# A delta-net stage whose TensorE order is planned at build time: three edits to the planner and one rank on VectorE

## The chip, the cores and the metric

The kernel runs on one core of one Trainium2 chip. The metric is the device time of one launch in microseconds (us); lower is better. TensorE (PE in the rows of the profile) does the matmuls, VectorE (DVE), ScalarE (ACT) and GpSimd (POOL) the elementwise work, and SyncE (SP) issues most of the DMAs. Each engine works through its own list of instructions in order.

## The reference, cut to what matters

A trunk of two layers over a sequence of 1024 rows of width 1024, all in f32. Each layer is a mixer and a convolutional FFN, each behind a modulation that is computed from a condition vector. The mixer of layer 0, which the change is about, is a gated DeltaNet with eight heads:

```python
e = jax.nn.silu(c @ cond_w + cond_b)
for i in range(DEPTH):
    mod = (e @ ada_w[i] + ada_b[i])[:, None, :]
    sh1, sc1, g1, sh2, sc2, g2 = jnp.split(mod, 6, axis=-1)
    y = mixers[i % N_MIXERS](x * (1.0 + sc1) + sh1)
    x = layer_norm(DN_ALPHA * x + (1.0 + g1) * y, ln_g[i, 0], ln_b[i, 0])
    y = conv_ffn(x * (1.0 + sc2) + sh2, ffn_up[i], ffn_conv_w[i], ffn_conv_b[i], ffn_down[i])
    x = layer_norm(DN_ALPHA * x + (1.0 + g2) * y, ln_g[i, 1], ln_b[i, 1])
...
# gated_deltanet, per head and chunk
qkv = jax.nn.silu(causal_dwconv(qkv, conv_w))
decay = jnp.where(causal, jnp.exp(jnp.where(causal, diff, 0.0)), 0.0)
kk = jnp.where(strict, jnp.einsum('bhncd,bhnmd->bhncm', kb, k) * decay, 0.0)
sol = lax.linalg.triangular_solve(kk + eye, rhs, left_side=True, lower=True, unit_diagonal=True)
qk = jnp.where(causal, jnp.einsum('bhncd,bhnmd->bhncm', q, k) * decay, 0.0)
_, o = lax.scan(step, state0, xs)
o = o * lax.rsqrt(jnp.mean(o * o, axis=-1, keepdims=True) + 1e-6) * norm_w
o = o * jax.nn.silu(z)
return o @ w_out
```

## The kernel before, in words

Products of two f32 operands in the projections are split into high and low parts and take three matmuls each (`wh`, `wl`, `hT`). The DeltaNet stage runs from about 88 to 640 us of the span. Its heads go in four pairs, with chunks of 128 rows (eight per head). The steps of a pair are generators, and a cooperative loop, `run` (L639), decides at build time in which order TensorE gets their matmuls: it keeps a modelled clock, `clk`, to which each matmul adds its cost, and a generator that yields a number is asked again when that much modelled time has gone by. The numbers are in the table `LAT` (how long the other engines or a DMA are expected to take); among the generators that are due, that with the lowest priority number goes next. `pq` (L625) pins this order for TensorE. On the other engines the instructions stand as a list scheduler puts them, which goes by priority.

The generators that matter here:

- `filler` projects q, k, v and z for all heads (128x512 matmuls `acc<-hT,wh` and `acc<-hT,wl`); their convolution ends on VectorE in L449. After each of its items it executes up to two *modulation steps*, if no solve is in its recursion (`busy`). A modulation step loads two pieces of 256 KB of `ada_w` (L213, into the two buffers `xT`) and adds them up on VectorE (`ada`, L221 for the first, L223 for the seven others). After four steps TensorE transposes the vector (L233), ScalarE sums it (L235, four) and VectorE adds the bias (L237 or L239). There are 24 such steps, six groups with eight VectorE operations each, for the modulation vectors 4, 3 and 2 of layer 0.
- `t_front` (pairs 0 to 3) makes the decay of a head (`decay`, with L740 on VectorE), writes it to DRAM (`Ld`, L751), and computes k times k for each half head: four matmuls into one of the two `mm` banks, then a chain of short VectorE operations on that bank, L766 to L776.
- `t_solve` inverts the diagonal 32x32 blocks, once for pairs 0 and 1 ("first solve") and once for pairs 2 and 3 ("second solve"): a recursion of 31 steps on VectorE, each L800 and L802, then the transposes L806 and L810 with ScalarE's copy L808 between them.
- `t_chain` of a pair copies the results apart on ScalarE (L849, L838) and then has TensorE combine the blocks, beginning with 32x32 matmuls `mm<-T,U`.
- `prep` transposes v and k (`mm<-cst,qkv`) and scales them on VectorE (L914, L923).
- `dt_half(p, q4)` loads half of a pair's decays back (L941, `DT<-Ld`, two loads), then yields `LAT["ld"]`, then does the matmuls of k and q (four per head, `mm<-qkv`), which VectorE multiplies with the loaded decay (L949). For `q4` of 0 the buffer is one of the four `lane` buffers, which the solve uses too.
- `scan` runs the recurrence over the chunks, and `tail` normalises its output.

Behind the stage come the gate (L1130), the gain row g1 (L1622 makes four diagonal matrices from half of modulation vector 2, L1623 turns them into rows, for each of the two halves) and the output projection (L327 to L329): 96 matmuls into the four accumulators for the first half of the columns, which VectorE empties with L357 (times g1), then the second half.

Of the kernel before, what the change touches and what calls it, by code (L numbers as in the profile page):

```python
# [12 lines left out]
ALU = mybir.AluOpType  # L13
# [14 lines left out]
ALPHA = 4.0 ** 0.25  # L28
BAL = {"r11": 0, "r12": 0, "r22": 0, "rS1": 0, "rS2": 0, "rS3": 0, "rS4": 0, "rw21": 0, "rwT1": 0, "rwT2": 0, "rwT3": 0, "rwT4": 0, "rn": 0, "rh": 1, "011": 0, "012": 0, "022": 0, "0S1": 0, "0S2": 0, "0S3": 0, "0S4": 0, "0w21": 0, "0wT1": 0, "0wT2": 0, "0wT3": 0, "0wT4": 0, "0n": 1, "0h": 0, "f11": 0, "f12": 0, "f22": 0, "fS1": 0, "fS2": 0, "fS3": 0, "fS4": 0, "fw21": 0, "fwT1": 0, "fwT2": 0, "fwT3": 0, "fwT4": 0, "fn": 1, "fh": 0, "gw": 0, "gh": 0, "gn": 3, "b1": 0, "b2": 0, "b3": 0, "b4": 0, "bT": 0, "ba": 0, "rw11": 0, "rw22": 0, "0w11": 0, "0w22": 0, "fw11": 0, "fw22": 0}
# [4 lines left out]
def trunk_kernel(ctx: ExitStack, tc, A):  # L34
# [645 lines left out]
    def q4s(q4):  # L680
        return slice(q4 * 4, (q4 + 1) * 4)
# [48 lines left out]
    def decay(h):  # L730
        for q4 in range(2):
            yield from take("t2", 2)
            gm = [tl("t2", [P, 4, P], F32R, name="gm") for _ in range(2)]
            for t, g in zip(gm, (gh64, gl64)):
                pool.tensor_tensor(t, bm(m_incl, 4), bc(g[:, q4s(q4), h], P), ALU.mult)
            yield LAT["gm"]
            pt = mm_tile()
            pm(pt, m_lowr, gm[1], start=True, stop=False)
            pm(pt, m_lowr, gm[0], start=False, stop=True)
            dve.tensor_tensor(U[h][:, q4s(q4)], v4(pt), bm(mneg, 4), ALU.add)  # L740
            give("t2", 2)

    def t_front(p):
        yield after_ev(("g",), ("Tq", p // 2 - 1))
        for h in pairs[p]:
            yield from take("aux", 1)
            U[h] = tl("aux", [P, NCH, P], name="U")
            yield from decay(h)
# [3 lines left out]
        for h in pairs[p]:  # L752
# [4 lines left out]
            for q4 in range(2):  # L757
# [5 lines left out]
                for c in range(4):  # L763
                    n = q4 * 4 + c
                    junk = tl("S", [P, P], name="jk")
                    dve.scalar_tensor_tensor(junk, pt[:, c * P:(c + 1) * P], 1.0, ident, ALU.mult, ALU.mult,  # L766
                                             accum_out=sk[:, n:n + 1])
                qs = q4s(q4)
                dve.tensor_scalar(sk[:, qs], sk[:, qs], 1e-6, None, ALU.add)
                dve.reciprocal(cj[h][:, qs], sk[:, qs])  # L770
                dve.tensor_tensor(cj[h][:, qs], cj[h][:, qs], beta[:, qs, h], ALU.mult)
                if q4:
                    pool.tensor_tensor(ir[h], sk, phalf, ALU.pow)
                for c in range(4):
                    n = q4 * 4 + c
                    dve.scalar_tensor_tensor(U[h][:, n], pt[:, c * P:(c + 1) * P], cj[h][:, n:n + 1],  # L776
                                             U[h][:, n], ALU.mult, ALU.mult)
# [149 lines left out]
    def dt_half(p, q4):  # L927
# [14 lines left out]
        yield LAT["ld"]  # L942
# [101 lines left out]
    busy, owed = [], [0]  # L1044

    def filler(items):
        spare = [(z, k) for k in range(GH)]
        todo = list(items)
        while todo or spare:
# [40 lines left out]
            for _ in range(0 if busy else min(owed[0], 2)):  # L1090
                bg_step(acc_tile)
                owed[0] -= 1

    LAT = {"kk": 3.05, "ld": 1.14, "g1": 17.30, "gm": 2.50, "mm": 1.81, "T": 4.98, "X": 3.38, "fs": 2.2, "T0": 5.00, "t1": 1.65, "t2": 2.35, "t3": 1.34, "D": 2.67, "s1": 1.60, "s2": 1.22, "s3": 1.26, "tail": 12.31, "ssq": 9.30, "fv": 2.85}
# [13 lines left out]
    run(todo)  # L1108
    zearly = list(range(GH))
# [883 lines left out]
```

## Time and profile before

| what | value |
|---|---|
| median of 3 runs | 2937.22 us (2934.47 to 2940.39) |
| the profiled execution: time, span | 2931.49 us, 2929.3 us |
| mean granted clock of TensorE | 0.989 of full speed |
| busy TensorE, VectorE, ScalarE | 2808.1, 2198.4, 1316.2 us |
| VectorE's idle time ahead of L223 (140 of them, all layers) | 27.0 us |

The profiled execution lies 5.7 us under the median. A row of the timeline has the start in the span and the length in us, engine, line, operation, output and inputs with buffer numbers left out, and how many instructions the row stands for; in brackets stands how long the engine was idle ahead of it and whose end released it. A row of waits has the sum in us, how often, and the longest. A row of grouped lines ends with busy time, the mean in ns, and the idle time ahead.

### The profile page before, as it was taken

Reading aid. Unit: us, or ns where it says so; the run is one execution under the profiler, and the core shown is the slowest. Engines: PE = TensorE matmul, PEld = TensorE weight load, DVE = VectorE, ACT = ScalarE, POOL = GpSimd, SP = SyncE. Lnnn points to the kernel's source line nnn. Section 1 sums busy time; section 2 is a strip of 40 time slices with the busy share of each in tenths; the row PEclk is TensorE's granted clock in tenths of the full one; section 3 lists DMA queues with packets and bytes.
Section 4 is the critical chain, followed back from the end, with each engine's and each line's share of the span. In section 5 each row is a group of like instructions: output and inputs, shape, how many; then the busy total and the mean of one; then the engine's idle time right before and its main releaser. Section 6 shows DMA issues by size and latency. Waiting matters only on the chain. (4 is left out here: it accounts for less than half of the span.)

```text
span 2929.3 us, 38823 instructions
## 1 busy us (share of the span) xinstructions
PE 2808.1 (96%) x13638; PEld 2296.3 (78%) x13638; DVE 2198.4 (75%) x3965; ACT 1316.2 (45%) x2457; POOL 421.1 (14%) x485
## 2 busy tenths in 40 slices
PE   8998999999999999999999999999999899999997
PEld 7777877887778888887787877777778688888786
DVE  6695687556788888897687766666697887778888
ACT  3755465443544444536443332221345544444443
POOL 0311220134011111100000000223201011111001
PEclk9999999999999999999999999999999999999999
DMA  8122221354344444863434454555564233335753
GB/s 309 64 80 80 98 91 44 105 187 148 108 150 159 163 157 147 316 218 123 157 110 173 149 181 149 165 172 163 189 235 155 94 137 108 108 108 202 262 158 119
DMA packets 239234, 442.35 MB, mean 151 GB/s; under 512 B 22848, under 2 KB 76352, under 8 KB 239040
## 3 DMA queue, kind: packets, MB, share of 16 engines
q1 hardware_dynamic: 206832, 387.96, 39.4%
q10 hardware_dynamic: 29760, 43.00, 4.0%
q0 software_dynamic: 2448, 8.91, 0.8%
q8 instruction: 107, 1.75, 0.2%
q14 instruction: 87, 0.71, 0.1%
HBM read 331.26 MB, written 108.53 MB: 150 GB/s over the span
## 5 line engine op out<-in xcount | busy, mean ns | idle before, releaser
L1466 PE MATMUL acc<-bb,ab 128*128 128x512 f32 x1800 | 427.5, 393 | 6.5 <-DVE pa L1441 2.5
L1466 PEld LDWEIGHTS acc<-bb,ab 128*128 128x128 f32 x1800 | 338.0, 189 | 81.4 <-DVE bb L90 3.8
L630 PE MATMUL acc<-hT,wh 128*128 128x512 f32 x960 | 300.3, 394 | 0.0
L1605 POOL TENSOR_TENSOR o<-o 128x512 f32<-128x512 f32 x88 | 121.1, 1387 | 810.6 <-DVE o L1598 680.4
L89 ACT ACTIVATE ab<-ar 128x512 fp32r<-128x512 f32 x210 | 129.0, 624 | 184.2 <-PE acc L1466 93.3
L1159 PE MATMUL acc<-T,wb 128*128 128x512 f32 x840 | 204.2, 392 | 7.2 <-DVE wb L90 7.2
L630 PEld LDWEIGHTS acc<-hT,wh 128*128 128x128 f32 x960 | 183.0, 191 | 34.0
L630 PE MATMUL acc<-hT,wl 128*128 128x512 f32 x480 | 202.8, 422 | 0.8 <-DVE qkv L993 0.5
L1159 PEld LDWEIGHTS acc<-T,wb 128*128 128x128 f32 x840 | 157.9, 189 | 43.7 <-DVE wb L90 11.1
L90 DVE TENSOR_TENSOR ab<-ar,ab 128x512 fp32r<-128x512 f32 x210 | 146.4, 703 | 44.2 <-ACT ab L89 44.2
L90 DVE TENSOR_TENSOR wb<-mm,wb 128x512 fp32r<-128x512 f32 x216 | 145.2, 684 | 23.4 <-ACT wb L89 21.7
L90 DVE TENSOR_TENSOR wb<-wr,wb 128x512 fp32r<-128x512 f32 x162 | 111.3, 688 | 65.7 <-ACT wb L89 63.8
L1225 ACT ACTIVATE pc<-acc 128x512 f32<-128x512 f32 x143 | 84.7, 592 | 160.5 <-PE acc L1159 91.6
L89 ACT ACTIVATE wh<-wr 128x1024 fp32r<-128x1024 f32 x101 | 107.0, 1061 | 110.2 <-PE acc L630 50.3
L89 ACT ACTIVATE wb<-mm 128x512 fp32r<-128x512 f32 x216 | 122.3, 593 | 72.8 <-DVE mm L1205 72.1
L90 DVE TENSOR_TENSOR wl<-wr,wh 128x1024 fp32r<-128x1024 f32 x85 | 105.5, 1241 | 61.2 <-ACT wh L89 59.1
L89 ACT ACTIVATE wb<-wr 128x512 fp32r<-128x512 f32 x162 | 99.7, 627 | 96.5 <-DMA wr<-in_ffn_up 53.0
L449 DVE SCALAR_TENSOR_TENSOR qkv<-raw,vc,qkv 128x512 f32<-128x512 f32 x144 | 112.3, 783 | 34.8 <-ACT qkv L447 30.7
L630 PE MATMUL acc<-wh,hT 128*128 128x512 f32 x384 | 135.5, 415 | 0.7 <-DVE vv L90 0.7
L1584 DVE SCALAR_TENSOR_TENSOR o<-g,vc,o 128x512 f32<-128x512 f32 (+2 forms) x176 | 135.2, 786 | 0.7
L223 DVE SCALAR_TENSOR_TENSOR ada<-mvw,e,ada 128x512 f32<-128x512 f32 x140 | 105.9, 757 | 27.0 <-DMA mvw<-in_ada_w 26.5
L110 PE MATMUL acc<-T,wb 128*128 128x512 f32 x292 | 116.6, 399 | 9.9 <-DVE wb L90 9.4
(626 smaller groups left out, 6876.5 us busy)
## 6 DMA issues: line engine op xcount, KB each, us to landing
wr<-in_ffn_up SPq DMA_DIRECT2D x96, 512.0 KB, 4.3
ad<-o SPq DMA_DIRECT2D x154, 256.0 KB, 2.2
ar<-ad SPq DMA_DIRECT2D x154, 256.0 KB, 4.2
mvw<-in_ada_w SPq DMA_DIRECT2D x48, 512.0 KB, 5.5
Br<-in_ffn_down SPq DMA_DIRECT2D x66, 256.0 KB, 3.3
mvw<-in_ada_w SPq DMA_DIRECT2D x64, 256.0 KB, 3.0
wr<-in_ret_wv SPq DMA_DIRECT2D x32, 512.0 KB, 4.2
ar<-od SPq DMA_DIRECT2D x56, 256.0 KB, 5.0
```

The source lines that it names most:

```text
L89: act.activation(dst_h, src, AF.Copy)
L90: eng.tensor_tensor(dst_l, src, dst_h, ALU.subtract)
L110: mm(acc, wl[:, k], hl[0], start=first, stop=False)
L223: dve.scalar_tensor_tensor(a, wr[kk], e[:, k:k + 1], a, ALU.mult, ALU.add)
L449: dve.scalar_tensor_tensor(oh, raw[:, 3 - j:515 - j], w[:, 3 - j:4 - j], oh, ALU.mult, ALU.add)
L630: pq(pe.matmul(out, lhsT, rhs, start=start, stop=stop, **kw), cost)
L1159: return pe.matmul(*a, skip_group_check=True, **kw)
L1225: act.activation(t, X, AF.Copy)
L1466: mm_ = (lambda *a, p=p, onto=onto, **kw: (mm if p < 2 else pe.matmul)(*a, skip_group_check=onto, **kw))
L1584: dve.scalar_tensor_tensor(tv, gv[:, c0 - j:c1 - j], w[:, 2 - j:3 - j], tv, ALU.mult, ALU.add)
L1605: pool.tensor_tensor(o[d], o[x], o[y], op)
```

## The change

Four edits. First, the table gets an entry `ld0` of 7.00, which `dt_half` yields after the loads of `q4` of 0 of the even pairs, in place of 1.14; so the planner puts these matmuls later. Second, a list `fronts` holds the fronts that are running, and `filler` executes no modulation step while it holds any. Third, the VectorE operations L740 and L766 to L776 (and GpSimd's power between them) are issued with a priority that is 80 higher, for the list scheduler. Fourth, modulation steps that are left when `run` ends are executed at once, ahead of the gate phase.

```diff
+RANK = 80
...
     def decay(h):
...
-            dve.tensor_tensor(U[h][:, q4s(q4)], v4(pt), bm(mneg, 4), ALU.add)
+            with tc.high_priority(RANK):
+                dve.tensor_tensor(U[h][:, q4s(q4)], v4(pt), bm(mneg, 4), ALU.add)
...
     def t_front(p):
         yield after_ev(("g",), ("Tq", p // 2 - 1))
+        fronts.append(p)
...
+                with tc.high_priority(RANK):
                     for c in range(4):
...
+        fronts.remove(p)
         emit(("A", p), LAT["kk"])
...
     def dt_half(p, q4):
...
-        yield LAT["ld"]
+        yield LAT["ld"] if p % 2 or q4 else LAT["ld0"]
...
-    busy, owed = [], [0]
+    busy, owed, fronts = [], [0], []
...
     def filler(items):
...
-            for _ in range(0 if busy else min(owed[0], 2)):
+            for _ in range(0 if busy or fronts else min(owed[0], 2)):
                 bg_step(acc_tile)
...
     run(todo)
+    while bg:
+        bg_step()
```

Line numbers of the changed kernel are higher: by 1 up to the first half of `decay`, by 2 to 7 behind it. What moves is shown at three places.

The first is TensorE's order around the first `mm<-T,U`, that of pair 0. Before, with all four groups of four `mm<-qkv` ahead of it (the second eight of them here):

```order
L630 MATMUL mm<-qkv 128x128 x8
L633 MATMUL mm<-cst,qkv 128x128 x8
L633 MATMUL acc<-cst,qkv 128x128 x8
L630 MATMUL acc<-hT,wl 128x512
L630 MATMUL acc<-hT,wh 128x512 x2
L633 MATMUL mm<-cst,qkv 128x128 x8
L630 MATMUL acc<-hT,wl 128x512
L630 MATMUL acc<-hT,wh 128x512 x2
L630 MATMUL acc<-hT,wl 128x512
L630 MATMUL acc<-hT,wh 128x512 x2
L630 MATMUL mm<-T_1923,U 32x32 x32
```

The same place after, with the second and the third group of four:

```order
L631 MATMUL mm<-qkv 128x128 x4
L634 MATMUL mm<-cst,qkv 128x128 x8
L631 MATMUL acc<-hT,wl 128x512
L631 MATMUL acc<-hT,wh 128x512 x2
L631 MATMUL acc<-hT,wl 128x512
L631 MATMUL acc<-hT,wh 128x512 x2
L634 MATMUL acc<-cst,qkv 128x128 x8
L631 MATMUL mm<-qkv 128x128 x4
L634 MATMUL mm<-cst,qkv 128x128 x8
L631 MATMUL acc<-hT,wl 128x512
L631 MATMUL acc<-hT,wh 128x512 x2
L631 MATMUL mm<-T_1896,U 32x32 x32
```

The groups of four have moved apart, and the fourth stands behind the `mm<-T,U`.

The second is VectorE's order where the second solve begins (`Y` is its transposed input, `fs` and `T` are the recursion's tiles). Before:

```order
L449 SCALAR_TENSOR_TENSOR qkv<-raw,vc,qkv 128x512
L792 STREAM_TRANSPOSE Y<-X 128x1024
L449 SCALAR_TENSOR_TENSOR qkv<-raw,vc,qkv 128x512
L800 TENSOR_TENSOR fs<-Y,T 128x31
L449 SCALAR_TENSOR_TENSOR qkv<-raw,vc,qkv 128x512
L802 TENSOR_TENSOR T<-T,fs 128x31
L449 SCALAR_TENSOR_TENSOR qkv<-raw,vc,qkv 128x512
L800 TENSOR_TENSOR fs<-Y,T 128x60
```

And after (L222 and L224 are the former L221 and L223, L805 and L807 the former L800 and L802):

```order
L238 SCALAR_TENSOR_TENSOR v_3820<-cs,vc 128x4
L222 TENSOR_SCALAR ada<-mvw,e 128x512
L797 STREAM_TRANSPOSE Y<-X 128x1024
L450 SCALAR_TENSOR_TENSOR qkv<-raw,vc,qkv 128x512
L224 SCALAR_TENSOR_TENSOR ada<-mvw,e,ada 128x512
L805 TENSOR_TENSOR fs<-Y,T 128x31
L450 SCALAR_TENSOR_TENSOR qkv<-raw,vc,qkv 128x512
L224 SCALAR_TENSOR_TENSOR ada<-mvw,e,ada 128x512
L807 TENSOR_TENSOR T<-T,fs 128x31
```

One group of modulation operations, which stood in the front of pair 3 before, now stands between the first steps of this recursion. The group that stood in the first solve has left it likewise.

The third is TensorE's order in the output projection (`hl` is the gated output, `dg` the diagonal matrices of the gain row). Before, at the projection's tenth matmul:

```order
L329 MATMUL acc<-wh,hl 128x512
L327 MATMUL acc<-wh,hl 128x512
L1623 MATMUL mm<-dg,ones 128x128 x4
L328 MATMUL acc<-wl,hl 128x512
L329 MATMUL acc<-wh,hl 128x512
```

After, behind the 96th:

```order
L329 MATMUL acc<-wl,hl 128x512
L330 MATMUL acc<-wh,hl 128x512
L234 MATMUL mm<-cst,ada 128x128 x4
L1630 MATMUL mm<-dg,ones 128x128 x8
L328 MATMUL acc<-wh,hl 128x512
L329 MATMUL acc<-wl,hl 128x512
```

The last modulation group (L234, the former L233) and the gain row that needs it have moved behind the first half.

More of the change, by code (lines that the diff above doesn't have):

```diff
@@ L762, in t_front @@
                     pm(pt[:, c * P:(c + 1) * P], ks, ks)
[L763 to L777, printed above, removed]
+                with tc.high_priority(RANK):
+                    for c in range(4):
+                        n = q4 * 4 + c
+                        junk = tl("S", [P, P], name="jk")
+                        dve.scalar_tensor_tensor(junk, pt[:, c * P:(c + 1) * P], 1.0, ident, ALU.mult, ALU.mult,
+                                                 accum_out=sk[:, n:n + 1])
+                    qs = q4s(q4)
+                    dve.tensor_scalar(sk[:, qs], sk[:, qs], 1e-6, None, ALU.add)
+                    dve.reciprocal(cj[h][:, qs], sk[:, qs])
+                    dve.tensor_tensor(cj[h][:, qs], cj[h][:, qs], beta[:, qs, h], ALU.mult)
+                    if q4:
+                        pool.tensor_tensor(ir[h], sk, phalf, ALU.pow)
+                    for c in range(4):
+                        n = q4 * 4 + c
+                        dve.scalar_tensor_tensor(U[h][:, n], pt[:, c * P:(c + 1) * P], cj[h][:, n:n + 1],
+                                                 U[h][:, n], ALU.mult, ALU.mult)
+        fronts.remove(p)
         emit(("A", p), LAT["kk"])
```

2 lines of the change are left out of this document (1 added, 1 removed).

## The prediction

> **What bounds the kernel now.** I read the page first, then the list of what TensorE waits for in the DeltaNet stage (85 to 700 us of the span), then the timeline around each of those waits, then the granted clock in slices of 4 us. From the page:
>
> ```profile
> PE 2808.1 (96%) x13638; PEld 2296.3 (78%) x13638; DVE 2198.4 (75%) x3965; ACT 1316.2 (45%) x2457; POOL 421.1 (14%) x485
> ```
>
> TensorE is the bound: it is busy 2808.1 of the 2929.3 us, and this change leaves its work as it is. So time can only be won or lost where TensorE stands still, or runs on a reduced clock. The longest waits in the stage are these (total, times, longest):
>
> ```profile
> PE mm L630 <- DVE DT L949: 8.2, 2, 5.6
> PE mm L630 <- DVE U L740: 5.0, 2, 4.1
> PE mm L630 <- DVE U L776: 4.2, 1, 4.2
> PE acc L327 <- DVE hl L90: 2.6, 1, 2.6
> ```
>
> The timeline of TensorE has the single waits; the bracket is the idle time ahead of the row and what ended it. The rows with `T,U 32*32` are the first matmuls of a pair's triangular chain ("T-chain" below), with no bracket: TensorE did not wait there.
>
> ```profile
> 134.49 1.93 PE L630 MATMUL mm<-qkv 128*128 128x128 f32 x8 [4.07 <-DVE U L740]
> 213.37 2.05 PE L630 MATMUL mm<-qkv 128*128 128x128 f32 x16 [1.51 <-DVE qkv L914]
> 216.20 0.66 PE L633 MATMUL mm<-cst,qkv 128*128 128x128 f32 x4 [0.79 <-DVE DT L949]
> 217.71 0.66 PE L633 MATMUL mm<-cst,qkv 128*128 128x128 f32 x4 [0.84 <-DVE qkv L914]
> 225.90 1.44 PE L630 MATMUL mm<-qkv 128*128 128x128 f32 x5 [5.59 <-DVE DT L949]
> 233.87 0.81 PE L630 MATMUL mm<-T,U 32*32 32x32 f32 x20
> 403.00 1.22 PE L630 MATMUL mm<-qkv 128*128 128x128 f32 x4 [4.16 <-DVE U L776]
> 473.59 0.66 PE L633 MATMUL mm<-cst,qkv 128*128 128x128 f32 x4 [0.78 <-DVE DT L949]
> 475.32 1.16 PE L630 MATMUL mm<-qkv 128*128 128x128 f32 x8 [0.38 <-DVE qkv L914]
> 479.12 1.61 PE L630 MATMUL mm<-qkv 128*128 128x128 f32 x7 [2.65 <-DVE DT L949]
> 486.87 0.24 PE L630 MATMUL mm<-T,U 32*32 32x32 f32 x2
> ```
>
> A wait costs more than itself where the clock falls after it. Columns: slice, its length and TensorE's busy time (matmuls), granted clock, DMA share, GB/s.
>
> ```profile
> 224.00:228.00 4.00, 2.10 (x10) 0.50 0.22 80
> 228.00:232.00 4.00, 4.00 (x24) 0.72 0.00 0
> 402.00:406.00 4.00, 3.00 (x11) 0.50 0.46 147
> 406.00:410.00 4.00, 4.00 (x15) 0.78 0.40 135
> 478.00:482.00 4.00, 2.88 (x13) 0.68 0.05 20
> 482.00:486.00 4.00, 4.00 (x19) 0.90 0.02 4
> 644.00:648.00 4.00, 3.71 (x20) 1.00 0.22 74
> ```
>
> Busy time times the missing clock gives what is lost: 2.10 x 0.50 + 4.00 x 0.28 = 2.2 us after the wait of 5.59 us, 2.4 us after that of 4.16 us, 1.3 us after that of 2.65 us, nothing after the 2.62 us at 644 us. With that these four waits cost 15.0 + 5.9 = 20.9 us, and not much more than that can be won here.
>
> **The change, place by place.** *First fronts (to 160 us).* The longest wait on L740, 4.07 us at 134 us, lies here. VectorE's order is the same before and after in its first 119 rows, which reach past this place: the rank moves nothing there. 0 us.
>
> *First solve, and the decay loads of pair 0* (first place shown with the change; the KQ matmuls, `mm<-qkv` with 128x128, are those whose results L949 multiplies with the loaded decays). The KQ matmuls come in fours with other work between them, the last four behind the T-chain, so I take it that the waits of 1.51 + 0.79 + 0.84 + 5.59 = 8.7 us and the 2.2 us of lost clock go, and TensorE by itself would reach the T-chain at 233.87 - 8.7 - 2.2 = 223.0 us. But the T-chain needs the copies L838, which hang on VectorE's 31-step recursion (last step L802) through two transposes and ScalarE:
>
> ```profile
> 220.02 0.19 DVE L802 TENSOR_TENSOR T<-T,fs 128x31 f32<-128x31 f32 x1
> 225.15 1.36 DVE L949 TENSOR_TENSOR DT<-DT,mm 128x512 f32<-128x512 f32 x2 [1.67 <-DMA DT<-Ld]
> 227.26 3.99 ACT L838 ACTIVATE T<-TX 32x256 f32<-32x256 f32 x6
> 472.71 0.18 DVE L802 TENSOR_TENSOR T<-T,fs 128x31 f32<-128x31 f32 x1
> 478.38 1.38 DVE L949 TENSOR_TENSOR DT<-DT,mm 128x512 f32<-128x512 f32 x2 [1.70 <-DMA DT<-Ld]
> 480.49 4.03 ACT L838 ACTIVATE T<-TX 32x256 f32<-32x256 f32 x6
> ```
>
> The copies end at 231.25 us, 11.0 us after the recursion; TensorE has 2.6 us of slack. What lets it come earlier is that the recursion ends earlier: eight modulation operations (one L221, seven L223) leave VectorE's queue there. Each takes 0.66 us start to start, L221 about 0.4:
>
> ```profile
> 399.47 0.75 DVE L223 SCALAR_TENSOR_TENSOR ada<-mvw,e,ada 128x512 f32<-128x512 f32 x1
> 400.13 0.75 DVE L449 SCALAR_TENSOR_TENSOR qkv<-raw,vc,qkv 128x512 f32<-128x512 f32 x1
> L223 DVE SCALAR_TENSOR_TENSOR ada<-mvw,e,ada 128x512 f32<-128x512 f32 x6 | 4.5, 745 | 1.4 <-DMA mvw<-in_ada_w 1.4
> 423.60:472.90 49.30, 45.16 (x100) 1.00 0.13 43
> ```
>
> So the copies end 7 x 0.66 + 0.4 = 5.0 us earlier, at 226.2 (third row: six of these operations in the first solve also waited 1.4 us for their loads, which would make it 6.4). TensorE then waits 3.2 us at the T-chain and starts it 7.6 us earlier. For the clock after a wait of 3.2 us the rows give 0 (644 us) to 2.4 us (403 us); I take 0.7, as it is nearest to the waits of 2.62 and 2.65 us. **-6.9 us**, between -4 (the last KQ wait stays in part) and -9. [...]
>
> *Front of pair 3.* The eight modulation operations that stood between the front's short ones on VectorE are gone from there, and one L449 that stood among them now stands behind. Three or four operations ahead of the L776 for which TensorE waited are thus 4 x 0.66 = 2.6 us of its 4.16 us; about 1.5 us stays, after which I expect no lower clock: 2.6 + 2.4 = 5.0 us, of which I keep 0.2 for the ones in its neighbourhood. **-4.8 us** (-2 to -6.5).
>
> *Second solve.* What left the fronts goes, in part, into VectorE's queue at the start of the second recursion (second place shown with the change). Before, no modulation operation stood between the front of pair 3 and the end of this recursion; now there are eight (5.0 us), and three more L449, three L914 and one L949 are ahead of its end too (7 at about 0.66, 4.6 us): 9.6 us. VectorE idled 49.3 - 45.2 = 4.1 us in that stretch, of which I let 3.5 be filled: the recursion, and the copies L838 with it, end 6.1 us later, at 484.52 + 6.1 = 490.6. TensorE, without its waits (0.78 + 0.38 + 2.65 us) and 1.3 us of lost clock, would be there at 481.8, so it waits 8.8 us, and starts the T-chain 3.8 us later than the 486.87 of before, then on half a clock (2.2 us as after 5.59 us). A gain at the decay load is more than given back: **+5.9 us**. The range is -1 if the operations only fill gaps and the 2.3 us of slack take the rest, +11 if nothing is filled and loads are waited for as in the first solve.
>
> *Gain row of the projection.* The last of the six groups of modulation steps is now built by the loop that drains the list, behind everything (third place shown with the change). Before, both groups of four `dg` matmuls stood among the first 30 matmuls of this projection. Now they follow all 96 of its first half, with all four accumulators full, and the second half needs an accumulator emptied by L357, which stands on VectorE behind the chain L235 (ScalarE), L237, L1622 x4:
>
> ```profile
> 162.32 0.16 DVE L237 SCALAR_TENSOR_TENSOR v<-cs,vc 128x4 f32<-128x4 f32 x1
> 395.69 0.27 ACT L235 ACTIVATE ada<-acc 128x128 f32<-128x128 f32 x1
> 396.59 0.23 ACT L235 ACTIVATION_READ_ACCUMULATOR ada<-acc 128x1 f32 x1
> 649.96 1.92 DVE L1622 TENSOR_SCALAR dg<-cst,v 128x128 f32<-128x128 f32 x4
> 664.89 0.69 DVE L357 TENSOR_TENSOR t<-acc,g 128x512 f32<-128x512 f32 x1 [11.02 <-PE acc L329]
> ```
>
> That is 1.1 (395.69 to 396.82, four of L235) + 0.2 + 1.9 + 0.7 = 3.9 us, all of it waited for, and about 1.1 us of clock (less than after 4.16 us, since small matmuls fall into the wait): **+5.0 us** (+2 to +8). It is hidden only if TensorE reaches L233 late for another reason.
>
> *The rest.* Sixteen modulation operations (10 us) move into the last scans, where VectorE has room; sixteen leave the first scans, where TensorE waited little:
>
> ```profile
> 560.00:600.00 40.00, 40.00 (x307) 36.21 (x307) 19.93 (x50) 17.16 (x46) 2.01 (x2) 1.00 0.40 133
> ```
>
> Here TensorE is 40.00 of 40 us busy, VectorE 19.93. 0 us (-1 to +3). On SyncE's queue the 256 KB loads now stand between the output projection's weights; each must wait for one of two buffers, but by the places of their readers on VectorE they come before the weights' own waits end.
>
> Sum: -6.9 - 4.8 + 5.9 + 5.0 = -0.8 us. The profiled execution took 2931.49 us (span 2929.3), so 2930.7; the median of the runs lies 5.7 us higher, and on that basis I predict 2936.4 us. A measurement of this kernel can tell about 0.2%, 5.9 us, from no change.
>
> **Rivals.** *Only the waits go* (faster): in the second solve VectorE has the 9.6 us to spare (place at -1) and the gain row costs 2 us. For it: 4.1 us of idle time and 2.3 us of slack there. Against it: the T-chain hangs on the recursion by 11 us of fixed work in both solves. -6.9 - 4.8 - 1 + 2 = -10.7, 2926.5 us; chance 0.34.
>
> *The second solve is held up by modulation loads* (slower): the eight operations share two buffers, the queue of SyncE is in order and has a weight load between them, so that VectorE waits for loads inside the recursion. If none of the 4.1 us is filled and 4 us of such waits are added, the place costs 9.6 + 4 - 2.3 + 2.2 = 13.5; with 5.0 for the gain row and 1 in the last scans, -11.7 + 19.5 = +7.8, 2945.0 us. It decides from the point where the copies L838 come over 13 us later, measured from the front's end. Against it: in the first solve six such operations waited only 1.4 us. Chance 0.20.
>
> *The load entry doesn't do what it says*: of pair 0, three of four KQ groups still stand ahead of the T-chain, and if L949 still holds a buffer there, the place wins 2.2 instead of 6.9 us. +3.9, 2941.1 us; chance 0.06.
>
> **The numbers.** My forecast has 0.40, most of it within 0.2%. Faster: 0.32 of the first rival and 0.04 of the forecast, 0.36; slower: 0.19 and 0.04, 0.23; the same 0.41. The forecast alone reaches from 2930 to 2943; to hold 8 in 10 the range takes in the middles of the rivals of both signs with some of their spread: 2923 to 2949.
>
> **What would show it.** Right: no wait on L949 over 2 us at 205 to 240 us; a T-chain of pair 2 that waits 6 to 11 us for L838 with a clock of about 0.5 behind it; a wait of about 4 us between L1623 and the projection's second half. Wrong: no wait at the T-chain of pair 2 (then it is faster), or waits of VectorE for modulation loads inside the second recursion (then slower), or a wait on L740 that is gone, since I give the rank there nothing.

## The result, and the profile after

The changed kernel takes 2951.97 us (median of 6 runs, 2946.21 to 2954.14) beside 2936.23 us of the kernel before in the same session (6 runs). The ratio is 1.0042, 95% interval 1.0030 to 1.0054: some 12 us slower, above the predicted range. The profiled execution took 2951.69 us, span 2949.3 us, mean granted clock 0.982 (before: 2931.49, 2929.3, 0.989). Profiled executions scatter: runs of one and the same kernel here differ by 5 to 16 us. So sizes of an edit come from the ratios below, each known to some 3 to 5 us, and places from the traces.

The page of the changed kernel: TensorE has the same 13,638 instructions and is 12.6 us longer busy, with equal work at the lower mean granted clock (0.982 beside 0.989).

```profile
PE 2820.7 (96%) x13638; PEld 2303.4 (78%) x13638; DVE 2202.6 (75%) x3965; ACT 1314.4 (45%) x2457; POOL 425.3 (14%) x485
```

TensorE's longest waits between 85 and 720 us of the changed kernel (total, times, longest):

```profile
PE mm L631 <- ACT T L843: 8.8, 2, 7.9
PE mm L631 <- DVE U L742: 5.1, 2, 4.1
PE mm L631 <- DVE qkv L919: 3.7, 2, 2.4
PE mm L1630 <- DVE dg L1629: 2.8, 1, 2.8
```

The decay load's wait (8.2 us on L949 before) has left the top; the wait of a triangular chain for its copies, 8.8 us on ScalarE's L843 (L838 before), is new. The timeline of TensorE shows where:

```profile
232.74 1.65 PE L631 MATMUL mm<-qkv 128*128 128x128 f32 x6 [2.43 <-DVE qkv L919]
242.57 2.08 PE L631 MATMUL mm<-T,U 64*64 64x64 f32 x32
394.06 1.28 PE L631 MATMUL mm<-qkv 128*128 128x128 f32 x8 [2.64 <-DVE U L780]
480.31 1.06 PE L631 MATMUL mm<-T,U 32*32 32x32 f32 x16 [7.94 <-ACT T L843]
482.25 2.58 PE L631 MATMUL mm<-T,U 32*32 32x32 f32 x48 [0.88 <-ACT T L843]
485.35 1.05 PE L631 MATMUL acc<-hT,wh 128*128 128x512 f32 x2
497.25 1.94 PE L631 MATMUL mm<-T,U 64*64 64x64 f32 x29
675.24 2.05 PE L1630 MATMUL mm<-dg,ones 128*128 128x128 f32 x8 [2.79 <-DVE dg L1629]
```

The rows `T,U 64*64` are the third step of a chain and serve as its mark below. In the kernel before they stand here:

```profile
243.18 2.02 PE L630 MATMUL mm<-T,U 64*64 64x64 f32 x31
496.18 1.02 PE L630 MATMUL mm<-T,U 64*64 64x64 f32 x14
```

How far the changed kernel is behind, at the start of one and the same matmul in both profiled executions (read from the timelines of TensorE):

| matmul | before | after | behind by |
|---|---|---|---|
| behind the wait on the first fronts' U (L740, L742) | 134.49 | 136.08 | 1.6 us |
| `T,U 64*64` of pair 0 | 243.18 | 242.57 | -0.6 us |
| `qkv` behind pair 3's front | 403.00 | 394.06 | -8.9 us |
| `T,U 64*64` of pair 2 | 496.18 | 497.25 | 1.1 us |
| first of the output projection | 644.29 | 645.70 | 1.4 us |
| first of the FFN behind it | 740.37 | 750.91 | 10.5 us |

So 9 us are won by 403 us, 10 are lost in the second solve, and 9 more in the projection. Of the 20 us at the end, 9.5 come behind the projection, where nothing was edited. That part, the same code in all sixteen kernels of this document, takes 2188.9 us in the trace before, 2198.4 in the one after, and 2188.9 to 2199.2 among the sixteen traces; so the 9.5 us are for the most part the luck of two executions, and the ratio of the medians has 12 us. Likewise the changed kernel is 2.25 us behind already at 88 us, where the stage begins. The second solve in the rows of VectorE and ScalarE (L797 begins the recursion, L807 is its last step, L843 the copies):

```profile
218.12 0.18 DVE L807 TENSOR_TENSOR T<-T,fs 128x31 f32<-128x31 f32 x1
225.61 3.96 ACT L843 ACTIVATE T<-TX 32x256 f32<-32x256 f32 x6
417.42 1.25 DVE L797 STREAM_TRANSPOSE Y<-X 128x1024 f32<-128x1024 f32 x1 [0.87 <-ACT X L793]
472.39 0.19 DVE L807 TENSOR_TENSOR T<-T,fs 128x31 f32<-128x31 f32 x1
479.63 3.86 ACT L843 ACTIVATE T<-TX 32x256 f32<-32x256 f32 x6
```

It takes 55.2 us from 417.42 to 472.58; before it ran from 426.58 to 472.89, 46.3 us:

```profile
426.58 1.25 DVE L792 STREAM_TRANSPOSE Y<-X 128x1024 f32<-128x1024 f32 x1 [0.40 <-ACT X L788]
```

### The profile page after: what moved, and what is told of

It reads as the page before. It is cut to its first block, busy times and chain, and to the rows that moved or that the text cites. A ratio compares the mean times of both kernels' runs of the same rounds, so it can differ in the third digit from the quotient of the medians.

```text
span 2949.3 us, 38836 instructions
## 1 busy us (share of the span) xinstructions
PE 2820.7 (96%) x13638; PEld 2303.4 (78%) x13638; DVE 2202.6 (75%) x3965; ACT 1314.4 (45%) x2457; POOL 425.3 (14%) x485
## 5 line engine op out<-in xcount | busy, mean ns | idle before, releaser
L1166 PEld LDWEIGHTS acc<-T,wb 128*128 128x128 f32 x840 | 158.0, 189 | 46.3 <-DVE wb L91 13.6
L90 ACT ACTIVATE wb<-wr 128x512 fp32r<-128x512 f32 x162 | 99.7, 626 | 98.8 <-DMA wr<-in_ffn_up 51.6
L224 DVE SCALAR_TENSOR_TENSOR ada<-mvw,e,ada 128x512 f32<-128x512 f32 x140 | 108.9, 778 | 29.3 <-DMA mvw<-in_ada_w 29.0
```

Source lines behind the costliest of these rows:

```text
L90: act.activation(dst_h, src, AF.Copy)
L224: dve.scalar_tensor_tensor(a, wr[kk], e[:, k:k + 1], a, ALU.mult, ALU.add)
L1166: return pe.matmul(*a, skip_group_check=True, **kw)
```

## The experiments

Three theories stood at first. **Theory 1:** the modulation steps, put into the second recursion and behind the projection by the gate, are the loss. **Theory 2:** the clock; a wait right ahead of the small matmuls of a chain halves it for long. **Theory 3:** the table entry `ld0` is the loss. A difference in us is the ratio's distance from 1, of 2937 us.

### The edits one by one

`e1_entry`, the entry alone, on the kernel before:

```diff
-        yield LAT["ld"]
+        yield LAT["ld"] if p % 2 or q4 else LAT["ld0"]
```

> Only the table entry for the decay loads, no gate on the modulation steps and no rank. Theory 1 (the loss comes from the modulation steps that the gate moves into the second solve and behind the projection): this kernel has no loss; the waits on L949 of 5.6 and 2.65 us go, but the chains' first matmuls then wait for the copies L838, which come as before, so only the slack of 2.6 and 2.3 us is won, and some clock: 3 to 7 us faster than before (about 2931). Theory 2 (what costs is a wait that is moved to stand right ahead of a chain's small matmuls, through the clock, whatever causes it): a half clock of more than 10 us behind the waits at both chains, 0 to 8 us slower than before (about 2940).

Measured: 2945.97 us, ratio 1.0028 (1.0018 to 1.0039): 8 us slower with this line alone. TensorE's timeline, and VectorE's groups within its first recursion (172.5 to 224.7 us):

```profile
235.41 1.06 PE L630 MATMUL mm<-T,U 32*32 32x32 f32 x16 [6.98 <-ACT T L838]
```

```profile
L914 DVE TENSOR_TENSOR qkv<-mm,ir 128x512 f32<-128x512 f32 x6 | 4.0, 680 | 0.0
L949 DVE TENSOR_TENSOR DT<-DT,mm 128x512 f32<-128x512 f32 x2 | 1.4, 680 | 0.1
```

The wait for the decay is gone, and one of 6.98 us for the copies has come. Two L914 and one L949 more than before stand in the recursion (4 and 1 there), which takes 52.1 us in place of 50.5. More is lost behind it, on ScalarE, whose rows are these before and in `e1_entry`:

```profile
220.25 1.96 ACT L808 ACTIVATE TP<-T 128x1024 f32<-128x1024 f32 x1 [5.02 <-DVE T L802]
222.11 5.13 ACT L849 ACTIVATE R<-RX 32x128 f32<-32x128 f32 x12
```

```profile
225.64 2.01 ACT L808 ACTIVATE TP<-T 128x1024 f32<-128x1024 f32 x1
228.99 0.75 ACT L447 ACTIVATE qkv<-acc,vc 128x512 f32<-128x512 f32 x1
229.56 5.14 ACT L849 ACTIVATE R<-RX 32x128 f32<-32x128 f32 x12
```

Before, L808 starts right behind the recursion (220.21 us) and the copies right behind L808. With the entry, other operations stand in ScalarE's list there (the squares L468 with their sums, L444, L447): 1.0 us ahead of L808 (the recursion ends at 224.66) and 2.0 us between L808 and the copies, which end 13.9 us behind the recursion in place of 11.0.

`e2_gate`, the gate with the drain behind `run`, without entry and rank:

```diff
+        fronts.append(p)
...
+        fronts.remove(p)
...
-            for _ in range(0 if busy else min(owed[0], 2)):
+            for _ in range(0 if busy or fronts else min(owed[0], 2)):
...
+    while bg:
+        bg_step()
```

> Only the gate on the modulation steps and the loop that drains them, no table entry and no rank. Theory 1 (the steps in the second solve and behind the projection are the loss): 8 to 16 us slower than before, 2944 to 2952, with the wait ahead of the second half of the projection unchanged (about 7 us there) and the second solve's copies as late as in the changed kernel. Theory 3 (the table entry is the loss): within 4 us of before, 2936.

Measured: 2937.42 us, 0.9996 (0.9986 to 1.0006). Theory 1 falls as the whole cause. The gate is level, although its modulation group is in the second recursion; what it wins it gives back: its trace is 13 us ahead of the kernel before at 437 us, 8 at pair 2's `T,U 64*64`, 5 at the projection's first matmul, and 5 us behind at the FFN's.

`e3_rank`, the rank alone (the list of modulation steps is empty when `run` ends):

```diff
-            dve.tensor_tensor(U[h][:, q4s(q4)], v4(pt), bm(mneg, 4), ALU.add)
+            with tc.high_priority(RANK):
+                dve.tensor_tensor(U[h][:, q4s(q4)], v4(pt), bm(mneg, 4), ALU.add)
...
```

> Only the rank of 80 on the front's short chain (and the loop that drains, which finds nothing left). Theories 1 to 3 alike: within 4 us of before; the wait of 4.07 us on the decay add at 134 us is still there, that of 4.16 us in the front of pair 3 is shorter by up to 1 us. If the rank were the cause of the loss, this kernel would be 8 us or more slower.

Measured: 2940.6 us, 1.0011 (1.0002 to 1.0020): 3 us, hardly more than can be told.

`h3_no_entry`, the changed kernel without the entry:

```diff
-        yield LAT["ld"] if p % 2 or q4 else LAT["ld0"]
+        yield LAT["ld"]
```

> The changed kernel without the table entry: gate and rank stay. If the entry is the cause: 2937 to 2942 us, the sum of the gate alone (level) and the rank alone (+3), with both chain phases back at 9.3 us. If the loss is in the gate's displaced modulation steps, or in several edits only together: 2948 to 2952.

Measured: 2940.06 us, 1.0005 (0.9993 to 1.0017). Without the entry the loss is gone, all but 1.5 us. `h4_entry_p0`, the entry for pair 0 alone:

```diff
-        yield LAT["ld"] if p % 2 or q4 else LAT["ld0"]
+        yield LAT["ld"] if p or q4 else LAT["ld0"]
```

> The changed kernel with the table entry for pair 0 alone; pair 2's order of decay loads and products is as without it. If the loss is at the second solve (the half clock of 20.5 us there): 2941 to 2945 us. If it is at the first chain: 2949 to 2952. If each chain's entry costs about alike, between: 2944 to 2948.

Measured: 2944.22 us, 1.0020 (1.0010 to 1.0029), between the two. So beside gate and rank the entry costs some 11 us, perhaps 4 of them at pair 0 and 6 at pair 2; each of these two differences is uncertain by some 5 us. Theory 3 stands, but it names an edit and no mechanism.

### Is it the clock?

`f1_entry_keep` puts matmuls, whose result nothing uses, into a wait of the entry alone; `h1_after_keep_more` has 10, 9 and 52 of them in the changed kernel, long enough to last until the copies are done, and `f2_after_keep` had 10 and 36:

```diff
+KEEP = {0: 30, 2: 6}
...
         yield from take("t2", 1)
+        if p in KEEP:
+            dm = sc_tile()
+            for _ in range(KEEP[p]):
+                pm(dm, ident_r, hT[1][0][0], cost=0.0)
```

> The table entry alone, with 30 matmuls of 128x512 of no use to the result ahead of the first chain's small matmuls (pair 0) and 6 ahead of pair 2's, all ready to run: they fill the waits of 7.0 and 1.25 us that the entry alone left there, and add nothing else. Theory 2 (what the entry costs is the clock, because its waits stand right ahead of small matmuls that don't bring the clock back): no half clock behind the chain of pair 0 at 231 to 245 us, and 6 to 10 us faster than the entry alone, that is from 4 us faster to 2 us slower than before (about 2936). Theory 3 in the plain form (the order that the entry makes is itself worse, whatever the clock): as slow as the entry alone, 6 to 11 us slower than before (about 2946).

Measured: 2942.12 us, 1.0009 (1.0000 to 1.0019), 6 us under the entry alone and between the two times that I had expected. The clock in slices, first of the entry alone, then with the wait filled:

```profile
236.00:240.00 4.00, 3.12 (x58) 0.50 0.00 0
240.00:244.00 4.00, 4.00 (x14) 0.50 0.00 0
```

```profile
236.00:240.00 4.00, 2.65 (x53) 0.92 0.00 0
240.00:244.00 4.00, 4.00 (x65) 0.66 0.00 0
```

The half clock is shorter. But measured from the recursion's start the `T,U 64*64` of pair 0 come after 76.0 us in place of 76.9: at the chain, only 0.9 us of the 6 show.

> The changed kernel, with 10 such idle-filling matmuls ahead of pair 0's chain (wait 2.4 us) and 36 ahead of pair 2's (wait 7.9 and 0.9 us). Theory 2: the 20 us of half clock from 477 us go, and with them some 8 to 10 us; 2940 to 2943. Theory 1 (the wait itself, from the modulation steps on VectorE, is the loss): no change beyond 2 us, about 2950.

Measured: 2950.7 us, 1.0040 (1.0025 to 1.0055): no gain. The filling ended at 483.11 us, ahead of the last copies (waits of 1.25 and 0.21 us behind it), and the half clock stayed: 0.50 from 488 to 500 us.

> The changed kernel with idle-filling 128x512 matmuls into a spare accumulator: 10 ahead of pair 0's first T,U step, 9 ahead of its first R,xa step, 52 ahead of pair 2's first T,U step, enough to last until the copies that the chains wait for are done. They compute nothing that is used. If the cost of the table entry is the half clock behind a wait among small matmuls (clock theory): no half clock of more than 6.8 us at either chain, chain phases of 10 to 12 us in place of 14.4 and 16.9, and 2942 to 2946 us, some 7 us under the changed kernel. If the cost lies in the order alone (the key and query products behind the first T,U step, the modulation steps in the second recursion): no gain, 2949 to 2953.

Measured: 2945.99 us, 1.0034 (1.0022 to 1.0046), which is 2.4 us under the changed kernel with intervals that overlap. Its clock and its timeline around pair 2's chain:

```profile
480.00:484.00 4.00, 4.00 (x53) 1.00 0.00 0
484.00:488.00 4.00, 4.00 (x95) 1.00 0.02 4
```

```profile
470.47 12.42 PE L633 MATMUL sc<-hT,ident_r 128*128 128x512 f32 x52
482.82 2.11 PE L633 MATMUL mm<-T,U 32*32 32x32 f32 x64
494.55 1.74 PE L633 MATMUL mm<-T,U 64*64 64x64 f32 x24 [2.60 <-DVE R L897]
```

The time lies at the upper end of what I had expected if the clock were the cause (2942 to 2946), and the chain from its first `T,U` to the 64x64 step takes 11.7 us, as that theory had it. But the gain in the ratio is 2.4 us and not 7. The clock is full, and yet the 64x64 step starts only 1.0 us earlier, measured from the recursion's start: now TensorE waits 2.60 us for VectorE's L897 there. That operation is late since two L452 and this L93 stand ahead of the chain's own operations in VectorE's list (L893 from 490.65 us on), and a third L452 among these:

```profile
489.40 1.22 DVE L93 TENSOR_TENSOR wl<-wr,wh 128x1024 fp32r<-128x1024 f32 x1
```

So of the 10 us lost in the second solve, the half clock accounts for 1.0 at most in this order, and Theory 2 falls as the main cause there.

### The modulation steps of the second recursion, and the gain row

`e5_late_gate`: the changed kernel, with a front counted only once it has its buffers, so that modulation steps run while it waits for them.

```diff
         yield after_ev(("g",), ("Tq", p // 2 - 1))
-        fronts.append(p)
         for h in pairs[p]:
             yield from take("aux", 1)
+            if p not in fronts:
+                fronts.append(p)
             U[h] = tl("aux", [P, NCH, P], name="U")
```

> The changed kernel, but a front counts as running only from when its first buffer is taken, not from when it stands in line for it; so the modulation steps run during the first scans again, none stands in either recursion on VectorE, and the gain row of the projection comes early as before. Theory 1: the second chain's wait of 8 us and the one of about 7 us in the projection go, 12 to 20 us faster than the changed kernel and 2 to 10 us faster than before (2926 to 2934). Theory 2: the gain in the projection alone, 6 to 9 us faster than the changed kernel (about 2943), with over 10 us of half clock at the second chain still.

Measured: 2940.41 us, 1.0009 (0.9999 to 1.0019), 10 us under the changed kernel. Its second recursion holds no modulation operation and takes 46.0 us, and no group is left behind `run`: its projection takes 97.5 us up to the FFN in place of 105.2. So Theory 1 wasn't all wrong: beside the entry, the groups that the gate puts into the second recursion and behind `run` cost. `f4_after_gain` builds vector 2 first and leaves the last group, which the gain row doesn't need then, behind it; `f5_gate_gain` does so with the gate alone:

```diff
+    bg_ada(0, 2, "col")
...
-    bg_ada(0, 2, "col")
...
-    while bg:
-        bg_step()
```

The loop stands behind the gain row instead.

> The changed kernel, with the modulation vector of the gain row built first of the three, and the loop that drains the rest put behind the gain row: the diagonal matmuls stand early in the projection again, as before. The wait of 2.8 us ahead of the projection's second half and the delay of 8.6 us that is seen across it should go: 5 to 9 us faster than the changed kernel (2943 to 2947). If the delay there is the late weights or the emptying of accumulators instead, under 3 us.

> The gate alone (no table entry, no rank), with the gain row's vector first and the drain behind it, as in the run before. The gate alone is level with before, its trace 3 us ahead of it at the projection's start and 5 us behind after it; if both hold, 5 to 9 us faster than the gate alone and than before (2929 to 2933). If the clock in other places takes it back, within 3 us of before.

Measured: 2949.39 us, 1.0041 (1.0029 to 1.0054), and 2939.69 us, 1.0002 (0.9992 to 1.0013). An early gain row wins nothing that can be told from zero: in `f4_after_gain` TensorE waits between the projection's halves for an accumulator instead (L328 for L358, 1.80 us), and then for split weights (L329, 1.06 us).

What the sixteen traces have in common says more. The stretch from the projection's first matmul to the FFN's first takes 96.0 to 97.7 us in the eight kernels in which no modulation step is left when `run` ends; TensorE is idle for 2.1 to 2.2 us of it and waits 0.8 us for split weights. In the eight in which a group is left it takes 103.5 to 107.9 us, with 6.4 to 9.1 us idle and 1.9 to 2.9 us of waits for split weights. `f4_after_gain` and `f5_gate_gain` are among these. So the loss in the projection goes with the group that is left, whether the gain row waits for it or not.

### VectorE's queue in the recursion

The runs so far have a number in common. For pair 2, from the start of the recursion: how long it takes, which operations stand in it that are not its own, how long behind it the copies L838 end, and how long behind these the 64x64 step starts (us; worked out from the rows of each profiled execution):

| kernel | recursion | modulation | L449 | L914, L949 | + copies | + 64x64 | sum |
|---|---|---|---|---|---|---|---|
| before | 46.3 | 0 | 25 | 2 | 11.6 | 11.7 | 69.6 |
| entry alone | 46.3 | 0 | 25 | 2 | 12.7 | 11.4 | 70.4 |
| gate alone | 51.7 | 7 | 25 | 3 | 11.1 | 12.1 | 74.9 |
| changed, without entry | 51.6 | 7 | 25 | 3 | 11.1 | 12.8 | 75.5 |
| changed, entry for pair 0 | 51.1 | 7 | 25 | 3 | 11.1 | 12.9 | 75.1 |
| changed | 55.2 | 7 | 28 | 6 | 10.9 | 13.8 | 79.9 |
| changed, waits filled (h1) | 55.2 | 7 | 28 | 6 | 11.6 | 12.1 | 78.9 |
| changed, late gate (e5) | 46.0 | 0 | 25 | 2 | 13.7 | 13.5 | 73.2 |

The two columns behind it move by some 3 us, the recursion by 9. **Theory 4:** a chain hangs on VectorE's list, where every operation that is put between the recursion's steps delays it by about its own length. VectorE is busy for 42.6 of the 46.3 us before and for 51.5 of the 55.2 us in the changed kernel: it is idle for 3.7 us in both, so all that was added lengthened the recursion. The gate puts seven L223 there; the entry, on top of the gate, six more (alone it puts none there, row 2). I take it that this is so since TensorE takes up transposes and projections in place of the products that wait for the decay, and their VectorE operations fall into the recursion. In `e5_late_gate`, where neither is there, the copies are late instead: as at pair 0 of the entry alone, other operations (L445, L448 and the four sums L236 of a modulation group) stand for 2.0 us between ScalarE's copy and the copies apart.

The sum is the place of the loss and not the whole time. The gate alone has 74.9 us in place of 69.6 and is level, as its recursion starts 13 us earlier and its projection is 10 us longer.

The groups in the recursion of the changed kernel (417.4 to 472.6 us), and those with the entry for pair 0 alone:

```profile
L450 DVE SCALAR_TENSOR_TENSOR qkv<-raw,vc,qkv 128x512 f32<-128x512 f32 x28 | 20.9, 746 | 0.2 <-ACT qkv L448 0.2
L224 DVE SCALAR_TENSOR_TENSOR ada<-mvw,e,ada 128x512 f32<-128x512 f32 x7 | 5.2, 749 | 2.3 <-DMA mvw<-in_ada_w 2.3
L919 DVE TENSOR_TENSOR qkv<-mm,ir 128x512 f32<-128x512 f32 x4 | 2.8, 688 | 0.0
L954 DVE TENSOR_TENSOR DT<-DT,mm 128x512 f32<-128x512 f32 x2 | 1.4, 685 | 0.0
```

```profile
L450 DVE SCALAR_TENSOR_TENSOR qkv<-raw,vc,qkv 128x512 f32<-128x512 f32 x25 | 18.6, 742 | 0.2 <-ACT qkv L448 0.2
L919 DVE TENSOR_TENSOR qkv<-mm,ir 128x512 f32<-128x512 f32 x2 | 1.4, 684 | 0.0
L954 DVE TENSOR_TENSOR DT<-DT,mm 128x512 f32<-128x512 f32 x1 | 0.7, 679 | 0.0
```

The six operations that the first has more are 2.3 + 1.4 + 0.7 = 4.4 us busy, and the recursion is 4.1 us longer. `k1_twice` tests this on the kernel before: each L800 of the second recursion is executed twice, with the same result.

```diff
-            dve.tensor_tensor(tv, bc(Y[:, j + 1:, j], nj), bm(T[:, j, 0:nj], ni), ALU.mult)
+            for _ in range(1 + qd_):
+                dve.tensor_tensor(tv, bc(Y[:, j + 1:, j], nj), bm(T[:, j, 0:nj], ni), ALU.mult)
```

> The kernel before with the multiplication of each step of the second recursion (L800) executed twice on VectorE, with the same result: 31 more operations of 0.18 to 0.45 us between the second solve's begin and its end, and nothing else. If the triangular chain hangs on VectorE's queue in the recursion (order theory): the recursion takes 54 to 56 us in place of 46.3, the copies end 8 to 9.5 us later, TensorE waits 5 to 7 us at the first T,U matmul of pair 2, and the time is 5 to 9 us above the kernel before. If the delay is made up again behind the solve, or the chain does not set the time: within 2 us of the kernel before. If the half clock behind a new wait were the main price, rather than the wait: 10 us or more above.

Measured: 2950.8 us, 1.0046 (1.0033 to 1.0058), 13.5 us slower. The group in its recursion, and its timeline:

```profile
L801 DVE TENSOR_TENSOR fs<-Y,T 128x31 f32<-128x31 f32 (+15 forms) x62 | 21.1, 340 | 1.5
```

```profile
428.55 1.25 DVE L792 STREAM_TRANSPOSE Y<-X 128x1024 f32<-128x1024 f32 x1 [0.40 <-ACT X L788]
487.56 0.19 DVE L803 TENSOR_TENSOR T<-T,fs 128x31 f32<-128x31 f32 x1
493.34 2.08 PE L630 MATMUL mm<-qkv 128*128 128x128 f32 x8 [14.78 <-DVE DT L950]
497.78 0.94 PE L630 MATMUL acc<-hT,wh 128*128 128x512 f32 x2
498.79 0.62 PE L630 MATMUL acc<-hT,wh 128*128 128x512 f32 x2
511.13 2.08 PE L630 MATMUL mm<-T,U 64*64 64x64 f32 x32
```

The recursion takes 59.2 us, 12.9 more; the 64x64 step comes 82.6 us behind its start, 13.0 more; the kernel is 13.5 us longer. The added operations came to more than the 8 to 9.5 us that I had taken, and TensorE waited at the decay product (L950, queued behind the recursion) and not at the chain. The time lies where I had expected it if the half clock were the main price (10 us or more); the trace decides against that, since 12.9 of the 13.0 us at the chain stand in the recursion. So the delay that was put in is the delay that comes out, and nothing was made up behind it.

`k2_twice_keep` is the same with 36 filling matmuls (as above, `KEEP = {2: 36}`).

> The same with 36 idle-filling 128x512 matmuls ahead of pair 2's first T,U matmul (8.3 us at full clock), which are done about when the copies are: no wait and no half clock there, the chain as late as in the other. Order theory: within 2 us of the other kernel, 4 to 8 us above the kernel before. Clock theory: at least 4 us under the other, at most 3 above the kernel before.

Measured: 2965.52 us, 1.0092 (1.0077 to 1.0108). This run missed its aim: since the wait was at L950, the filling stood behind it, and 8.59 us of matmuls simply came on top (`sc<-hT,ident_r` at 502.78 us, the chain at 511.30). It says nothing on the clock; beside `k1_twice`, it shows that work ahead of a chain that is not waiting costs its whole length: the 64x64 step comes 9.0 us later, and the kernel is 13.5 us slower by the ratios, which are uncertain by some 6 us here.

### A version that beats both

`h2_late_gate_only`: the gate of `e5_late_gate`, without entry and rank, on the kernel before. Nothing stays in the second recursion, and the gain row is built early.

```diff
+            if p not in fronts:
+                fronts.append(p)
...
+        fronts.remove(p)
...
-            for _ in range(0 if busy else min(owed[0], 2)):
+            for _ in range(0 if busy or fronts else min(owed[0], 2)):
```

> Only the gate, counted after a front has its buffers, with neither the table entry nor the rank: the chain order is as before. If the entry is the loss and the gate's gains around the fronts are real: 2927 to 2932 us, 5 to 10 under the kernel before. If what the gate gains is given back later whatever is done: 2935 to 2940.

Measured: 2932.24 us, 0.9985 (0.9976 to 0.9994): 4.4 us faster than the kernel before, a little less than expected, and about 17 faster than the changed one. Its second recursion:

```profile
416.39 1.25 DVE L798 STREAM_TRANSPOSE Y<-X 128x1024 f32<-128x1024 f32 x1 [1.06 <-ACT X L794]
462.28 0.18 DVE L808 TENSOR_TENSOR T<-T,fs 128x31 f32<-128x31 f32 x1
```

46.1 us, as before, and its start has come 10 us earlier. Of these 10 us its trace has 9.3 left at pair 2's `T,U 64*64` and 0.7 at the projection. Two of its modulation groups stand in the last scans, where the kernel before has one; that they are what costs there was not tested.

## Why the prediction was wrong, step by step

The three signs that were to show the prediction right came: no wait for a decay over 2 us at 205 to 240 us (the longest is 1.40), a wait of 8.8 us at pair 2's chain with a clock of 0.50 behind it, and a wait at L1630 ahead of the projection's second half, of 2.8 us where I had about 4. The mechanisms were there, but their prices were wrong. The two gains, forecast as 6.9 + 4.8 = 11.7 us, came to 3.0 + 8.3 = 11.3 in the traces. That the sum fits is luck, as both terms are wrong and the errors cancel. The two losses, forecast as 5.9 + 5.0 = 10.9 us, came to 10.0 + 9.1 = 19.1. These two are the steps that failed.

**First fronts, rank: right.** The wait on L740 (now L742) stands as it was, 4.07 us. The rank alone measured 3 us of loss against the 0 of the prediction, at the edge of what can be told.

**First solve: less than half in size.** The waits for the decays went, and so did the modulation operations: the recursion ended 1.9 us earlier (218.30 beside 220.21) although TensorE was 2.4 us late at 160 us, so 4.3 us (forecast 5.0). The sum had -6.9 for the place; it gave -3.0. The step that failed is "TensorE has 2.6 us of slack": I credited the start of the first T,U matmuls, 7.6 us earlier. Behind them TensorE now has the products that the entry moved there, which wait for 2.43 us (232.74) and are followed by 128x512 matmuls on a reduced clock (0.50 from 232 to 236 us; 1.05 us for two at 235.04), and the 64x64 step comes 13.0 us behind the copies in place of 11.9. The gate alone won 5.4 us at this place (`e2_gate`), and the entry alone lost 3.4 (`e1_entry`): what I had booked as the gain of the entry was a loss.

**First scans and pair 3's front: more than forecast.** Forecast was 0 and -4.8; together -8.3 came (-0.6 to -8.9 in the table), of which some 6 ahead of 380 us. The wait on L776 fell from 4.16 to 2.64 us (forecast 1.5). That moving sixteen modulation operations out of the first scans would win nothing, since TensorE showed little idle time, was wrong: the gate alone won 6.4 us there up to 380 us, the entry alone nothing. It isn't their number, as `h2_late_gate_only` has two groups in these scans too, at other places, and won 5.2 us.

**Second solve: the failed step.** Forecast +5.9, measured 10.0 to 10.2. The direction, the wait (8.8 us forecast; 7.94 + 0.88) and the clock of 0.50 behind it were right. Two sizes were not. One is the idle time of VectorE, "4.1 us in that stretch, of which I let 3.5 be filled": the recursion became 8.8 us longer, not 6.1. Nothing was filled; VectorE is idle for 3.7 us in the recursion before and after. In the changed kernel 2.3 of them are waits of L224 for loads (row above), but these are not the reason: with 0.8 us of such waits (`h1`) the recursion takes the same 55.2 us. The other is the "2.3 us of slack": with T,U started 0.3 us behind the copies and at full clock, the next step still waited 2.60 us for VectorE (`h1`). So the slack that I saw in TensorE's rows was none of the chain's in this order. Together these two make 2.7 + 2.3 us of the error, less 0.7 us by which the copies followed the recursion sooner (10.9 us in place of 11.6).

**Gain row: the second failed step.** Forecast +5.0, of it 3.9 of waiting; the wait at L1630 was 2.79 us, but the stretch from the projection's first matmul to the FFN lost 9.1. TensorE is idle for 7.7 us of it in place of 2.2, and busy for 3.6 us longer at a mean clock of 0.98 in place of 1.00. That small matmuls in the wait would keep the loss of clock behind it at 1.1 us was my estimate; no run tested the reason, and the size fits (0.61 and 0.97 in the slices from 674 and 678 us, 2.76 x 0.39 + 4.00 x 0.03 = 1.2 us). Beside the gain row's 2.8 us it waits 2.9 us for split weights (0.8 before) and 1.4 us for an accumulator that ScalarE empties with L1087 (a projection of z). So I had priced the gain row's wait and put the rest of the group that is left at nothing, its loads above all, which were to come "before the weights' own waits end". With the gain row built early, the projection was about as long (103.5 us in `f4`, 105.2 in `f5`). Which of the group's parts, the loads, the VectorE operations or the accumulator, costs how much was not tested.

**Last scans:** 0 forecast. TensorE lost 2.4 us more there, but 2.1 of them only took the place of its wait for the gated output (2.62 us before, 0.51 after).

**The rivals.** The slower one, modulation loads that hold up the second solve, was nearest in time (2945.0). Half of its mechanism was there, that none of the idle time is filled; the other half, 4 us of added waits for loads, was not: 2.3 us of them came, in place of other idle time. That the entry might be a loss by itself was in no case. I had counted it as the gain of a wait. The entry moved TensorE's products only, so I looked for its price on TensorE; as far as the traces place it, it lay in other operations that came into the lists of VectorE and ScalarE ahead of the chain.

What stays open: the entry alone costs 8 us, of which its trace places 3.4 at pair 0's chain (1.6 in the recursion and 2.9 on ScalarE, less 1.0 behind the copies) and 1 at pair 2's; the rest lies within the scatter of profiled executions. With the filled wait (`f1`) 6 us came back, of which 0.9 were seen at the chain, so for the entry alone a part of the clock in the loss is not excluded.

## What to carry to other kernels

When a planner postpones a consumer on one engine, look at what is brought forward in its place, and into which other engine's list its follow-up work falls: here six VectorE operations of 0.7 us lengthened the second serial recursion by 4.1 us, more than the 3.8 us of waits that were removed there. Idle time ahead of a chain is no slack of the chain until the chain's own last producer has been followed, and gaps in a serial stretch are not room for foreign work: this recursion kept its 3.7 us of idle time and grew by all that was put in. When background work is held back, follow it to where it runs instead; holding it back until a front has its buffers, rather than from when the front stands in line, kept it out of the recursions and from behind the stage, and won 4.4 us.

## What the runs showed of the hardware

The half clock that stands at pair 2's chain, with its 32x32 matmuls, lasts long in the changed kernel (slice, length and TensorE's busy time, granted clock, DMA share, GB/s):

```profile
480.00:484.00 4.00, 2.81 (x53) 0.50 0.01 4
484.00:488.00 4.00, 4.00 (x24) 0.50 0.00 0
488.00:492.00 4.00, 4.00 (x97) 0.50 0.02 4
492.00:496.00 4.00, 4.00 (x18) 0.50 0.48 131
496.00:500.00 4.00, 3.95 (x40) 0.83 0.00 0
```

TensorE counts as busy from 482 us on, with two stretches of 128x512 matmuls among it, 4 us from 484.75 and 3 us from 492.26 (1.05 us for two at 485.35, beside 0.62 at 436.58 at a granted clock of 1.00), and the clock comes back only in the slice from 496 us, some 14 us later. In `k1_twice`, where 128x128 and 128x512 matmuls alone follow a wait of 14.78 us, two 128x512 take 1.05 us at 496.50, 0.94 at 497.78 and 0.62 at 498.79: by these lengths the clock is full again about 5 us behind the restart. Whether the 32x32 matmuls are what made the half clock of the changed kernel last longer, no run here tested alone.
